# Split instead of unsplit weights for the second half of the K tiles in the first four projection groups of a hybrid decoder trunk

## The chip, the core and the metric

The kernel runs on one core of one Trainium2 chip. The metric is the device time of one execution in microseconds, the median of several executions. TensorE is called PE, its weight loads PEld, VectorE DVE, ScalarE ACT, GpSimd POOL, and SyncE SP; SP issues nearly all loads from HBM.

## What is computed

Two layers of a decoder trunk on a sequence of 256 tokens with a model width of 2048, in float32. Each layer normalizes and modulates its input, multiplies it with one wide input projection, mixes the heads in four different ways, projects back, and adds a gated feed-forward part. Only the start of layer 0 matters here:

```
mod = cond @ w_ada[l] + b_ada[l]
sh1, sc1, g1, sh2, sc2, g2 = jnp.split(mod[:, None, :], 6, axis=-1)
h = rms_norm(x, norm_gain[l, 0]) * (1.0 + sc1) + sh1
w_proj = w_in[l] if l == 0 else jnp.concatenate([w_in[l], vres_down[l - 1]], axis=1)
p = h @ w_proj
...
y_mix = jnp.concatenate([y_a, y_b, y_c, y_d], axis=-1) @ w_out[l]
x = x + g1 * y_mix
...
x = x + g2 * ((jax.nn.silu(gate) * up) @ ffn_w2[l])
```

`cond` is one vector, so `mod` is 12288 dot products of length 2048 per layer.

## The kernel before

The width of 2048 is cut into 16 K tiles of 128. For each K tile `h` exists in two forms. `hh` and `hl` are its high and low part in the fp32r type, made by ACT (`hh`) and DVE (`hl`); a product of two split operands is three fp32r matmuls (hh x hi, hl x hi, hh x lo). `u` is the unsplit h in float32, used for one float32 matmul in place of the three.

Weights come in *pieces* of 128 x 1024: two K tiles of a group of 512 output columns. An unsplit piece is loaded into a tile called `whole` and used as it lies. A split piece is loaded, two at a time, into a tile called `raw` (1 MB, three buffers); ACT copies it into `hi` (method `conv`), DVE subtracts to get `lo` (method `lower`). `hi` and `lo` have four buffers each, which the `whole` tiles share. `conv` for the piece three ahead is emitted at the first K tile of a piece (`LEAD` is 3), `lower` soon after:

```python
nc.scalar.activation(hi[:, :n], raw, AF.Copy)
...
nc.vector.tensor_tensor(lo, raw, hi[:, :n].bitcast(F32), ALU.subtract)
```

Layer 0 begins in `start_quads`, which multiplies while `h` is still being made. For each K tile of h, four tiles `ar` of 128 x 1024 of the modulation weights `wada` are loaded (two halves each for scale and shift; five buffers), DVE multiplies each with `cond` and sums (a *dot*, method `ada_dot`), adds the bias (two or three tiny operations on `mod`) and makes `u` from x; ACT adds the shift to `u` and makes `hh`; DVE makes `hl`. One dot is emitted every one to three K tiles of matmuls, or more when a K tile of h is asked for that isn't there yet. The three stages of `start_quads`, in order:

- Stage 1: four groups named in `ONE` on K tiles 0 to 7, unsplit. The result is parked in `sp`.
- Stage 2: the groups lo, k, r and v (`TWO`) on K tiles 0 to 7, split, one group after the other.
- Stage 3: the same four groups on K tiles 8 to 15, into the same four accumulators (`q`, `q`, `m`, `m`: two PSUM banks each). The pieces go round the four groups, two K tiles at a time. Unsplit pieces are taken four at a time (`g = 4`): the four groups on the first K tile, then on the second.

When a group ends, ACT and DVE shift it out of PSUM into `sh` tiles. After stage 3 come the narrow group lo2, the rest of the `ONE` groups (which are split), and the other groups, between which a planner lays the work of the head mixers. It orders by its own clocks per engine, so a change of one stage's operations also moves later rows against each other.

The engines run their instructions in the order in which the program emits them, and SP issues its loads in that order too, each one when its buffer is free. The recording helper makes every instruction appear under line 181.

Of the kernel before, what the change touches and what calls it, by code (L numbers as in the profile page):

```python
# [15 lines left out]
KT = D // 128  # L16
# [15 lines left out]
ONE, TWO, KA = ("q" + GROUPS[0], "k" + GROUPS[0], "v" + GROUPS[0], "q" + GROUPS[1]), ("lo", "k", "r", "v"), 8  # L32
# [5 lines left out]
def weight_plan():  # L38


    plan = []
    count = itertools.count()

    def put(src, l, groups, ks, nk=None, beside=False, whole=False):

        out = []
        for j, (name, cols) in enumerate(groups):
            n = sum(c for _, c in cols)
            k = nk or max(i for i in (2, 4, 8) if i * n <= 1024)
            i = next(count)  # L50
            out.append([dict(src=src, l=l, name=name, quad=i, k0=k0, nk=k, cols=cols, n=n, whole=j in whole if isinstance(whole, tuple) else whole)
                        for k0 in ks if k0 % k == 0])
        for g in zip(*out) if beside else out:
            plan.extend(g)

    for l in range(L):
        lo = 3 * GW
        g0 = lo + 192
        base = NIN - 9 * GW
        cols = dict(lo=[(lo, 96), (g0, 32), (lo + 96, 96), (g0 + 32, 32), (g0 + 64, 256)],  # L60
                    lo2=[(g0 + 320, 128)] + ([(NIN, 64)] if l else []),
                    k=[(GW, GW)], r=[(0, GW)], v=[(2 * GW, GW)])
        for g in GROUPS:
            i = "BCD".index(g)
            for w, t in enumerate("qkv"):
                cols[t + g] = [(base + (3 * i + w) * GW, GW)]
        allk = range(KT)
        if l == 0:
            one, two = [(n, cols[n]) for n in ONE], [(n, cols[n]) for n in TWO]
            put("in", l, one, range(KA), beside=True, whole=True)  # L70
            put("in", l, two, range(KA))
            put("in", l, two, range(KA, KT), beside=True, whole=True)
            put("in", l, [("lo2", cols["lo2"])], allk)
            put("in", l, one, range(KA, KT))
            put("in", l, [(n, c) for n, c in cols.items() if n not in ONE + TWO + ("lo2",)], allk)
        else:
            put("in", l, list(cols.items()), allk)
        outs = [(f"o{q}", [(q * 512, 512)]) for q in range(4)]
        for g in (outs[:2], outs[2:]):
            for i, part in enumerate(WO[:2]):  # L80
                put("w_out", l, g, part, whole=i in PLAIN[l])
        put("w_out", l, outs, WO[2], whole=2 in PLAIN[l])
        f0 = 0
        for c in CHUNKS:
            fs = [(f"f{p}", [(p * 128, 256), (DFF + p * 128, 256)]) for p in range(f0, f0 + c, 2)]
            if f0 == 0:
                put("w13", l, fs[:4], allk, beside=True)
                fs = fs[4:]
            put("w13", l, fs, allk)
            put("w2", l, [(f"p{q}", [(q * 512, 512)]) for q in range(4)], range(f0, f0 + c))  # L90
            f0 += c
    units, off, i = [], 0, 0
    while i < len(plan):
        m = i
        w = 0
        while m < len(plan) and plan[m]["whole"] == plan[i]["whole"] and w + plan[m]["nk"] * plan[m]["n"] <= (1024 if plan[i]["whole"] else UNIT):
            plan[m].update(unit=len(units), at=w)
            w += plan[m]["nk"] * plan[m]["n"]
            m += 1
        units.append((off, w, i, m))  # L100
        off += 128 * w
        i = m
    return plan, units, off
# [108 lines left out]
class Kern:  # L212
    def __init__(self, tc, nc, I, out, ctx, cfg):
# [14 lines left out]
        self.dr = en(tc.tile_pool(name="dr", bufs=1, space=bass.MemoryType.DRAM))  # L228
        self.uid = 0
        self.plan, self.units, _ = weight_plan()  # L230
        self.adae = getattr(self.nc, cfg.get("adae", "sync"))
        self.next_dma = self.next_conv = self.pos = 0
# [1594 lines left out]
def prepare(inp):  # L1827
# [5 lines left out]
    d["c"] = np.ascontiguousarray(g["c"])  # L1833
    d["wada"] = np.ascontiguousarray(g["w_ada"].transpose(0, 2, 1).reshape(L, 96, 128, D))
    plan, units, total = weight_plan()
    wst = np.empty(total, np.float32)
    src = {}
# [71 lines left out]
```

## Time and profile before

| | |
|---|---|
| median of 3 runs | 2596.36 us (2595.82 to 2599.79) |
| the profiled execution | 2601.3 us, of which the span of the trace is 2599.4 us |
| PE, DVE, ACT busy over the span | 97%, 70%, 44% |
| DMA over the span | 252 GB/s |
| stage 3 | from 140.6 to 196.6 us of the span |

The profiled execution took 1.9 us more than its span, and lies 4.9 us above the median of the runs. A busy PE isn't PE at its peak: matmuls overlap, so the distance from start to start is what one costs.

### The profile page before, as it was taken

The numbers are of one execution on the slowest core, as the hardware profiler recorded it, in microseconds if no ns is written. First come the engines' busy times: TensorE is split into PE (matmuls) and PEld (weight loads), VectorE is DVE, ScalarE is ACT, GpSimd is POOL, SyncE is SP. The second block draws the span as 40 slices with busy tenths as digits, with TensorE's granted clock in tenths as the row PEclk, the third lists the DMA queues.
The fourth block names the chain that finished last, engine by engine and source line by source line (L and its number), as shares of the span: only waits on it lengthen the run. The fifth ranks groups of instructions, "written<-read, shape, count | busy, mean of one in ns | idle before, by whom it ended". The sixth has DMA issues, their size and how long they took to land.

```text
span 2599.4 us, 37374 instructions
## 1 busy us (share of the span) xinstructions
PE 2522.2 (97%) x14550; PEld 2162.3 (83%) x14550; DVE 1810.8 (70%) x2934; ACT 1133.4 (44%) x1602; POOL 153.0 (6%) x270
## 2 busy tenths in 40 slices
PE   7999999999999999999999999999899999999998
PEld 4888888887888888888899998989788888888887
DVE  6766887859877887865567878889754455545555
ACT  2315445414444434433455454566444444444343
POOL 0001122010000000000020012100100000000001
PEclk9999999999999999999999999999899999999999
DMA  9895688878898888865577786787455555555553
GB/s 352 314 375 199 212 271 267 312 266 323 322 345 325 323 331 329 319 243 185 180 257 273 261 280 227 261 306 262 146 181 193 193 194 190 192 186 193 179 194 114
DMA packets 136019, 654.70 MB, mean 252 GB/s; under 512 B 18581, under 2 KB 24749, under 8 KB 88609
## 3 DMA queue, kind: packets, MB, share of 16 engines
q1 hardware_dynamic: 126306, 632.72, 67.1%
q0 software_dynamic: 8960, 18.55, 2.4%
q8 instruction: 114, 1.87, 0.3%
q10 hardware_dynamic: 576, 1.05, 0.1%
q14 instruction: 63, 0.52, 0.1%
HBM read 643.82 MB, written 10.77 MB: 252 GB/s over the span
## 4 chain that ended last, share of the span: by engine, by line
PE 89%; DMA 5%; DVE 4%; ACT 2%; issue 1%; POOL 0%; SPq 0%; DVEq 0%; ACTq 0%; POOLq 0%
PE q L181 75%; PE m L181 13%; DMA ar<-wada 2%; DVE ar L181 1%; DMA gb<-gate 1%; DVE lo L181 1%; DMA raw<-wst 0%; DVE x L181 0%; ACT hi L181 0%; PE st L181 0%; DMA XT<-scr 0%; DMA whole<-wst 0%; DVE rstd L181 0%; DVE out L181 0%; ACT sh L181 0%
## 5 line engine op out<-in xcount | busy, mean ns | idle before, releaser
L181 DVE TENSOR_TENSOR lo<-raw,hi 128x1024 fp32r<-128x1024 f32 (+1 forms) x742 | 904.4, 1226 | 504.7 <-ACT hi L181 504.2
L181 ACT ACTIVATE hi<-raw 128x1024 fp32r<-128x1024 f32 (+1 forms) x742 | 780.7, 1058 | 923.9 <-PE q L181 762.0
L181 DVE SCALAR_TENSOR_TENSOR ar<-ar,cond 128x1024 f32<-128x1024 f32 x384 | 464.2, 1223 | 54.4 <-DMA ar<-wada 53.6
L181 PE MATMUL q<-hi,hh 128*128 128x512 f32 x1456 | 456.0, 394 | 7.0 <-ACT hh L181 6.8
L181 PE MATMUL q<-lo,hh 128*128 128x512 f32 x1456 | 453.4, 393 | 0.0
L181 PE MATMUL q<-hi,hl 128*128 128x512 f32 x1456 | 450.6, 391 | 0.0
L181 PEld LDWEIGHTS q<-hi,hl 128*128 128x128 f32 x1456 | 274.3, 188 | 58.8 <-issue 0.4
L181 PEld LDWEIGHTS q<-hi,hh 128*128 128x128 f32 x1456 | 270.2, 189 | 62.7 <-ACT hh L181 7.9
L181 PEld LDWEIGHTS q<-lo,hh 128*128 128x128 f32 x1456 | 272.2, 188 | 57.3 <-issue 1.5
L181 PE MATMUL q<-hh,hi 128*128 128x256 f32 (+1 forms) x1040 | 176.2, 289 | 5.9 <-ACT hh L181 3.4
L181 PE MATMUL q<-hh,lo 128*128 128x256 f32 (+1 forms) x1040 | 177.0, 290 | 2.7 <-DVE lo L181 2.6
L181 PE MATMUL q<-hi,ah 128*128 128x512 f32 x576 | 178.3, 391 | 0.0
L181 PE MATMUL q<-lo,ah 128*128 128x512 f32 x576 | 178.2, 391 | 0.0
L181 PE MATMUL q<-hi,al 128*128 128x512 f32 x576 | 177.5, 389 | 0.0
L181 PE MATMUL q<-hl,hi 128*128 128x256 f32 (+1 forms) x1040 | 171.2, 284 | 0.0
L181 PEld LDWEIGHTS q<-hh,hi 128*128 128x128 f32 (+1 forms) x1040 | 145.8, 193 | 13.7 <-issue 5.7
L181 PEld LDWEIGHTS q<-hh,lo 128*128 128x128 f32 (+1 forms) x1040 | 145.4, 192 | 8.6 <-issue 3.5
L181 PEld LDWEIGHTS q<-hl,hi 128*128 128x128 f32 (+1 forms) x1040 | 144.8, 192 | 0.1
L181 POOL TENSOR_TENSOR sq<-sq,sq 128x256 f32<-128x256 f32 x44 | 36.2, 822 | 1680.6 <-ACT sq L181 1678.1
L181 PEld LDWEIGHTS q<-hi,al 128*128 128x128 f32 x576 | 108.1, 188 | 22.6
L181 PEld LDWEIGHTS q<-lo,ah 128*128 128x128 f32 x576 | 107.5, 188 | 22.0
L181 PEld LDWEIGHTS q<-hi,ah 128*128 128x128 f32 x576 | 107.4, 188 | 21.8
(270 smaller groups left out, 2644.1 us busy)
## 6 DMA issues: line engine op xcount, KB each, us to landing
raw<-wst SPq DMA_DIRECT2D x369, 1024.0 KB, 5.0
ar<-wada SPq DMA_DIRECT2D x384, 512.0 KB, 6.7
whole<-wst SPq DMA_DIRECT2D x64, 512.0 KB, 7.6
x<-xt SPq DMA_DIRECT2D x32, 128.0 KB, 4.0
bias<-bskew POOLq DMA_DIRECT2D x24, 128.0 KB, 6.9
bskew<-bscr POOLq DMA_DIRECT2D x4, 576.0 KB, 19.5
gb<-gb POOLq DMA_DIRECT2D x16, 128.0 KB, 5.9
xd<-x POOLq DMA_DIRECT2D x16, 128.0 KB, 5.9
```

The source lines that it names most:

```text
L181: return f(*a, **kw)
```

## The change

One flag falls. The pieces of stage 3 are split ones, as in stage 2; `beside=True` stays, so they still go round the four groups, each piece with its two K tiles.

```diff
             put("in", l, one, range(KA), beside=True, whole=True)
             put("in", l, two, range(KA))
-            put("in", l, two, range(KA, KT), beside=True, whole=True)
+            put("in", l, two, range(KA, KT), beside=True)
             put("in", l, [("lo2", cols["lo2"])], allk)
```

On PE, the first rows of stage 3, before. `u_564` and `u_792` are h on K tiles 8 and 9, the numbers behind `whole` those of the pieces of lo, k, r and v:

```order
L181 MATMUL q_213<-u_564,whole_923 128x256 x4
L181 MATMUL q_214<-u_564,whole_984 128x256 x4
L181 MATMUL m_215<-u_564,whole_1019 128x256 x2
L181 MATMUL m_216<-u_564,whole_1019 128x256 x2
L181 MATMUL m_217<-u_564,whole_1045 128x256 x2
L181 MATMUL m_218<-u_564,whole_1045 128x256 x2
L181 MATMUL q_213<-u_792,whole_923 128x256 x4
```

And now:

```order
L181 MATMUL q_213<-hh_565,hi_986 128x256 x4
L181 MATMUL q_213<-hl_634,hi_986 128x256 x4
L181 MATMUL q_213<-hh_565,lo_987 128x256 x4
L181 MATMUL q_213<-hh_793,hi_986 128x256 x4
L181 MATMUL q_213<-hl_846,hi_986 128x256 x4
L181 MATMUL q_213<-hh_793,lo_987 128x256 x4
L181 MATMUL q_214<-hh_565,hi_1023 128x256 x4
```

Three matmuls stand where one stood, and group lo takes both K tiles before group k starts.

On DVE, in the middle of stage 3, before: the four dots (`ar`) of K tile 12, its `u_1150` and `hl_1164`, with nothing else between them:

```order
L181 SCALAR_TENSOR_TENSOR ar_1083,mod_73<-ar_1083,cond 128x1024
L181 SCALAR_TENSOR_TENSOR mod<-mod_73,vecs 128x1
L181 SCALAR_TENSOR_TENSOR mod<-mod,vecs 128x1
L181 SCALAR_TENSOR_TENSOR ar_1092,mod_73<-ar_1092,cond 128x1024
L181 SCALAR_TENSOR_TENSOR ar_1099,mod_73<-ar_1099,cond 128x1024
L181 SCALAR_TENSOR_TENSOR mod<-mod_73,vecs 128x1
L181 SCALAR_TENSOR_TENSOR u_1150<-x_110,mod,rstd_200 128x256
L181 SCALAR_TENSOR_TENSOR ar_1112,mod_73<-ar_1112,cond 128x1024
L181 TENSOR_TENSOR hl_1164<-u_1150,hh_1151 128x256
```

The same K tile now (`u_1236`, `hl_1260`):

```order
L181 TENSOR_TENSOR lo_1202<-raw_1122,hi_1201 128x1024
L181 SCALAR_TENSOR_TENSOR ar_1120,mod_73<-ar_1120,cond 128x1024
L181 SCALAR_TENSOR_TENSOR ar_1141,mod_73<-ar_1141,cond 128x1024
L181 SCALAR_TENSOR_TENSOR mod<-mod_73,vecs 128x1
L181 SCALAR_TENSOR_TENSOR u_1236<-x_110,mod,rstd_200 128x256
L181 TENSOR_TENSOR lo_1242<-raw_1122,hi_1241 128x1024
L181 SCALAR_TENSOR_TENSOR ar_1162,mod_73<-ar_1162,cond 128x1024
L181 TENSOR_TENSOR hl_1260<-u_1236,hh_1237 128x256
```

Sixteen `lo` have come between the dots. `lo_1242` stands right behind `u_1236`.

On ACT, the same place, before:

```order
L181 ACTIVATE u_1102<-u_1102,mod 128x256
L181 ACTIVATE hh_1103<-u_1102 128x256
L181 ACTIVATE u_1150<-u_1150,mod 128x256
L181 ACTIVATE hh_1151<-u_1150 128x256
L181 ACTIVATE u_1190<-u_1190,mod 128x256
```

And now:

```order
L181 ACTIVATE hi_1201<-raw_1122 128x1024
L181 ACTIVATE u_1236<-u_1236,mod 128x256
L181 ACTIVATE hh_1237<-u_1236 128x256
L181 ACTIVATE hi_1241<-raw_1122 128x1024
L181 ACTIVATE hi_1281<-raw_1199 128x1024
```

The copy `hi_1241`, which PE and `lo_1242` need, stands behind `u_1236` and `hh_1237`, which need the dots of K tile 12. On SP, seven loads of 1 MB into `raw` stand where fourteen of 512 KB into `whole` stood ahead of the last `ar` of the stage; an eighth follows it.

## Rows read from the trace of the kernel before

**Rows 1.** Busy time by stretch: length, busy time (instructions), PE's granted clock, DMA share, GB/s.

```profile
98.00:140.60 42.60, 41.52 (x344) 41.12 (x343) 30.91 (x46) 16.59 (x20) 0.00 (x0) 1.00 0.72 263
140.60:196.60 56.00, 55.79 (x258) 48.33 (x256) 33.18 (x70) 9.73 (x19) 2.80 (x7) 1.00 1.02 399
```

**Rows 2.** The chain of waits, 98 to 220 us: start, length, what.

```profile
149.62 8.55 DMA ar<-wada
...
189.70 3.47 PE q L181 x16
193.19 0.48 ACT sh L181
...
218.17 1.94 PE q L181 x14
```

**Rows 3.** PE in order of time: start, length, operation, count, idle before and releaser.

```profile
140.16 0.64 PE L181 MATMUL m<-hh,lo 128*128 128x256 f32 x4
140.64 3.62 PE L181 MATMUL q<-u,whole 128*128 128x256 f32 x16
...
192.99 3.62 PE L181 MATMUL m<-u,whole 128*128 128x256 f32 x16
198.09 0.39 PE L181 MATMUL q<-hh,hi 128*128 128x256 f32 x1 [1.49 <-DVE sh L181]
```

**Rows 4.** DVE's groups, 136 to 187.5 us: count | busy, mean ns | idle before, releaser.

```profile
L181 DVE SCALAR_TENSOR_TENSOR ar<-ar,cond 128x1024 f32<-128x1024 f32 x21 | 25.4, 1221 | 13.5 <-DMA ar<-wada 13.5
L181 DVE SCALAR_TENSOR_TENSOR mod<-mod,vecs 128x1 f32<-128x1 f32 x16 | 3.2, 200 | 0.6
L181 DVE TENSOR_TENSOR hl<-u,hh 128x256 fp32r<-128x256 f32 x6 | 2.5, 422 | 1.0 <-ACT hh L181 1.0
```

**Rows 5.** DVE in order of time, stages 2 and 3.

```profile
99.90 3.50 DVE L181 TENSOR_TENSOR lo<-raw,hi 128x1024 fp32r<-128x1024 f32 x3 [1.97 <-ACT hi L181]
103.32 1.22 DVE L181 SCALAR_TENSOR_TENSOR ar<-ar,cond 128x1024 f32<-128x1024 f32 x1
...
113.48 1.23 DVE L181 TENSOR_TENSOR lo<-raw,hi 128x1024 fp32r<-128x1024 f32 x1 [3.59 <-ACT hi L181]
...
120.76 2.36 DVE L181 TENSOR_TENSOR lo<-raw,hi 128x1024 fp32r<-128x1024 f32 x2 [1.97 <-ACT hi L181]
...
132.54 1.23 DVE L181 TENSOR_TENSOR lo<-raw,hi 128x1024 fp32r<-128x1024 f32 x1 [3.22 <-ACT hi L181]
...
135.96 1.22 DVE L181 SCALAR_TENSOR_TENSOR ar<-ar,cond 128x1024 f32<-128x1024 f32 x1
...
183.18 0.43 DVE L181 TENSOR_TENSOR hl<-u,hh 128x256 fp32r<-128x256 f32 x1 [1.02 <-ACT hh L181]
```

**Rows 6.** ACT in order of time, one K tile of stage 2.

```profile
118.82 0.51 ACT L181 ACTIVATE u<-u,mod 128x256 f32<-128x256 f32 x1 [4.42 <-DVE u L181]
119.36 0.42 ACT L181 ACTIVATE hh<-u 128x256 fp32r<-128x256 f32 x1
119.69 1.99 ACT L181 ACTIVATE hi<-raw 128x1024 fp32r<-128x1024 f32 x2
```

**Rows 7.** PE in stage 1, two rounds of the same sixteen matmuls.

```profile
33.56 3.72 PE L181 MATMUL q<-u,whole 128*128 128x256 f32 x16 [1.56 <-ACT u L181]
...
84.29 5.41 PE L181 MATMUL q<-u,whole 128*128 128x256 f32 x16 [3.43 <-ACT u L181]
```

**Rows 8.** Busy time by stretch, as rows 1, around a wait of PE.

```profile
84.00:86.00 2.00, 1.71 (x4) 1.44 (x5) 0.34 (x1) 1.97 (x4) 0.00 (x0) 0.59 0.96 346
86.00:88.00 2.00, 2.00 (x6) 1.59 (x6) 1.22 (x2) 0.58 (x1) 0.00 (x0) 0.56 1.05 385
88.00:90.00 2.00, 2.00 (x10) 1.56 (x9) 1.36 (x2) 0.86 (x2) 0.00 (x0) 1.00 0.97 377
```

**Rows 9.** PE's two waits after stage 3.

```profile
218.17 0.74 PE L181 MATMUL q<-hh,lo 128*128 128x256 f32 x4 [2.64 <-DVE lo L181]
...
268.30 4.56 PE L181 MATMUL m<-sh,up 32*128 32x256 f32 x10 [3.42 <-DVE kar L181]
```

## The prediction, as put on record before the change was run

> **What bounds the kernel now.** The page first: PE is busy for 97% of the span, so time lost or won on PE stays lost or won to the end, unless a later wait of PE swallows it. The busy time by stretch comes next [rows 1]. In stage 3 PE is busy for 55.8 of 56.0 us at a granted clock of 1.00, DMA is full at 399 GB/s, DVE works 33.2 us and ACT 9.7 us. Whoever reads only this sees a PE-bound stage with two idle engines. The chain of waits corrects that: it enters stage 3 through PE, but also through a load of `ar` of 8.55 us [rows 2]. So behind PE a second chain runs nearly as late, that of h: loads of `ar`, dots on DVE, `u`, `hh`, `hl`. DVE's groups show it [rows 4]: of the stretch from the first dot of the stage (135.96 us) to the last `hl` (183.61 us) [rows 5], 47.6 us, DVE waited 13.5 us for `ar`, 1.0 for `hh` and 0.6 for small things, and worked 32.5 us. PE took the last K tile at about 189.7 us [rows 2], so h was ready some 6 us before it was needed. That is the whole slack.
>
> **The change part by part.** *PE.* Sixteen unsplit records follow each other in 3.46 us, and the stage has 256, so it costs 56 us (140.64 to 196.6, [rows 3]). Four split matmuls take 0.48 us from start to start [rows 3], so one piece on one K tile takes three times that, 1.44 us; 32 of these are 46.1 us. Taken alone that is a gain of 9.9 us, with an end at 186.7 us.
>
> *DVE.* Sixteen `lo` are added. Three in a row take 3.42 us until the next row starts, 1.14 us each [rows 5]: 18.2 us. With the 32.5 us there already, DVE has 50.7 us of work, more than PE's 46.1. DVE runs in its own order, and the order shows 14 of the 16 `lo` ahead of the last `u`, the first ahead of the first dot. So with no wait at all the last `u` is done at 135.96 + 32.5 - 0.4 (the last `hl`) + 14 x 1.14 = 184.1 us. The gain of 9.9 us is thereby excluded: DVE can't deliver the last K tile of h in time for it.
>
> *ACT.* Sixteen `hi` of about 1.0 us are added [rows 6] to an engine with 46 us to spare [rows 1]; hidden as work, not as order. Stage 2 already has the new pattern: a `u` on DVE, then `u` and `hh` on ACT, then `hi` on ACT, and DVE's next row is the `lo` of that `hi`. Twice DVE stood idle 1.97 us there [rows 5], which is what ACT needs for `u`, `hh` and `hi` [rows 6]. Before, nothing like it stands in stage 3; now three K tiles (10, 12 and 13) have `lo` straight behind `u`: 3 x 1.97 = 5.9 us. Last `u`: 190.0 us. Behind the waiting `lo` stand the next dots, and behind these, on SP, the loads that want their buffers.
>
> *Late data.* The bytes hardly change: `raw` in place of `whole`. But a dot that runs later frees its `ar` buffer later, and SP, which issues in order, now also waits for a `raw` buffer, which is free only after a `lo`. How much DVE then waits for loads is not in the trace. Below it is nothing: DVE, itself later, finds all `ar` landed. Above it is the 13.5 us that it waited in this stage [rows 4]. The nearest row is stage 2, which has this mix of dots and `lo`: no wait for `ar`, but 3.59 and 3.22 us for `hi` whose load was late [rows 5], 6.8 us at 263 GB/s. I take 6.8: the last `u` is done at 196.8 us, and `hh`, after `u` and `hh` on ACT [rows 6], 1.0 us later, at 197.8 us.
>
> *The end of the stage.* PE has by then done lo on K tile 14 and waits. Left are lo on K tile 15 and k, r and v on both, seven times 1.44 = 10.1 us: 207.9 us.
>
> *The clock.* A wait of that length has a price. After PE had waited 3.43 us, the granted clock stood at 0.59 and 0.56 for the next 4 us, near its lower level (1.2 GHz of 2.4) [rows 8], and the round that followed took 5.41 us in place of 3.72 [rows 7], 1.7 us more; after 2.64 us [rows 9] no loss shows. I add 1.7: 209.6 us, 13.0 us later than before. The Trainium skill ("TensorE: Matmul & The Clock Gate", section "HAM oscillation — how this bites in real kernels") goes further: in a loop in which every K tile waits for its data, PE falls back to the half clock in each wait and every K tile starts cold. By it all of the last 10.1 us would run at half speed, and the sum would be 8.4 us higher than by the rows. The rows agree that a wait costs clock, but show full speed again within the second round.
>
> *What comes back.* Before, the four groups ended within 6 us of each other, and PE then waited 1.49 us for lo's `sh` to leave its accumulator [rows 3] and 2.64 us for a `lo` that stood on DVE behind the shifting of all of them and the start of the mixers [rows 9]; the chain of waits runs through this from 193 to 218 us [rows 2]. Now each group ends 2.9 us after the one before it, lo 8.6 us ahead of the end, and most is shifted out by then: I take back 1.5 us of the first and 1.0 of the second. Bounds: nothing, and 4.1. Further on PE waits 3.42 us at 268 us [rows 9], behind POOL's loads and stores. In the new order the little matmul that starts POOL's table (`oh`, `rb`) stands about 4 us of PE's work earlier; I take back 1.5, between 0 and 3.4. After that the planner's rows are the same work in a shifted order; I count nothing for it, and some 3 us either way.
>
> Sum: +13.0 - 1.5 - 1.0 - 1.5 = +9.0 us. On the profiled execution, 2601.3 us, that is 2610.3; on the median of the runs, 2596.4, it is **2605.4 us**, which I forecast. A measurement tells 0.2% here, 5.2 us, from no change.
>
> **The rivals.**
> - *DVE never waits.* The loads come in time, and ACT and DVE overlap so that no `lo` waits: last `u` 184.1, `hh` 185.1, end 195.2 us, -1.4, and with the 4.0 us that come back -5.4: 2591.0 us. For it: DMA has fewer bytes per us to bring once DVE is the slower. Against it: the 1.97 us waits, which the order repeats. It is decided by the last `hh`: below about 190.5 us there the kernel gets faster. 0.11.
> - *Order costs, data doesn't.* The three waits of 1.97 us stay, no load is late, PE's wait is too short for the clock: 190.0 + 1.0 + 10.1 = 201.1, +4.5 - 4.0 = +0.5: 2596.9 us. For it: no dot waited for `ar` in stage 2. Against it: stage 2 asks for a dot once in some three K tiles of matmuls, about 10 in its 42 us, stage 3 for 21 [rows 4] in little more. 0.20.
> - *The loads stay as late as they were.* All 13.5 us remain beside the new work: 216.3, +19.7 - 4.0 = +15.7: 2612.1 us. For it: each late dot delays the buffer for a later one. Against it: DVE would be idle 19 us while fewer loads per us are wanted. 0.09.
> - *Cold to the end of the stage.* The last wait drops the clock until the stage ends: +9.0 + 8.4 = +17.4: 2613.8 us. For it: the drop itself [rows 8]. Against it: the recovery in the same rows. [...] 0.07.
>
> **How the numbers follow.** The forecast has the remaining 0.53, with 2600 to 2610 as its own range. Faster by over 0.2% is the first rival alone: 0.11. Within 0.2% are the second rival and a little of the forecast's lower end: 0.20 + 0.06 = 0.26. Slower: 0.63. From 2594.5 to 2613 the range leaves out the first rival and the upper half of the last ones, 0.18.
>
> **What would show it.** In the trace after, stage 3 still starts at 140.6 us and ends near 209. Four split matmuls still take 0.48 us, with PE busy well under 50 us of some 68. DVE's `ar` group shows far less than 13.5 us of waits for DMA, its `lo` group 10 to 15 us for ACT's `hi`. PE's longest wait is for `hh` of the last K tile, over 4 us, with a granted clock near half behind it. DMA falls clearly below 399 GB/s. The prediction is wrong if the last `hh` comes before 190 us, if PE waits in the stage less than 10 us in total, or if the waits at 218 and 268 us grow by more than they are taken to shrink.

## The result and the profile after

The changed kernel takes 2627.5 us (median of four runs, 2626.3 to 2632.7), the kernel before beside it 2598.1 (2595.8 to 2604.1): a ratio of 1.0102, 95% interval 1.0084 to 1.012. That is slower, as forecast, but by 29 us and not by 9, and 14.5 us above the upper end of the range. The profiled execution took 2626.4 us, its span 2624.7, so 25.3 us more than the span before. The ratio on record lies a little below the quotient of the two medians, 1.0113; versions are compared by their ratios from here on.

Busy time by stretch, in the columns of [rows 1]; the second stretch is stage 3, which now ends at 207.8 us and ended at 196.6:

```profile
98.00:140.60 42.60, 41.52 (x344) 41.11 (x343) 29.40 (x41) 17.91 (x22) 0.00 (x0) 1.00 0.76 278
140.60:207.80 67.20, 53.07 (x385) 51.45 (x384) 52.97 (x89) 24.81 (x35) 2.79 (x7) 0.90 0.82 300
```

PE is no longer full (53.1 of 67.2 us, at a mean granted clock of 0.90), DMA fell from 399 to 300 GB/s, and DVE went from 33 us of work to 53. The chain of waits through the stage (start, length, what) no longer runs through loads of `ar`. It is DVE and ACT handing work to each other, and in two places a load of `raw`; a stretch of PE from 165 to 169 us, left out here, belongs to it too:

```profile
150.61 7.22 DMA raw<-wst
157.91 1.07 ACT hi L181
159.00 1.23 DVE lo L181
...
162.69 0.49 DVE u L181
163.20 0.52 ACT u L181
163.74 0.42 ACT hh L181
164.16 0.95 ACT hi L181
...
178.81 8.24 DMA raw<-wst
187.14 1.07 ACT hi L181
188.23 1.23 DVE lo L181
...
192.19 1.14 DVE lo L181
193.33 1.15 DVE ar L181 x2
194.51 0.22 DVE mod L181
194.73 0.41 DVE u L181
195.16 0.52 ACT u L181
195.70 0.42 ACT hh L181
196.17 6.08 PE q L181 x36
```

SP issued these two loads of `raw` right behind loads of `ar` that had waited for DVE (issued at 150.19 and 178.29 us in the same chain). So DVE's lateness comes back to DVE as a late `hi`.

DVE's groups from 136 to 198 us, beside [rows 4]: the dots (`ar`) wait for nothing, where they waited 13.5 us for loads, and the new `lo` wait 10.4 us for ACT's high part:

```profile
L181 DVE SCALAR_TENSOR_TENSOR ar<-ar,cond 128x1024 f32<-128x1024 f32 x21 | 25.4, 1219 | 0.0
L181 DVE TENSOR_TENSOR lo<-raw,hi 128x1024 fp32r<-128x1024 f32 x15 | 18.4, 1224 | 11.5 <-ACT hi L181 10.4 <-PE q L181 1.1
```

PE in order of time, beside [rows 3] and [rows 9]. Four split matmuls take 0.48 us from start to start at full clock; after the wait of 4.46 us they take 0.81 to 0.86 for a while. The last rows are the wait for lo's accumulator and the two waits behind it:

```profile
196.17 0.73 PE L181 MATMUL q<-hh,hi 128*128 128x256 f32 x4 [4.46 <-ACT hh L181]
196.74 1.01 PE L181 MATMUL q<-hl,hi 128*128 128x256 f32 x4
...
198.41 1.06 PE L181 MATMUL q<-hh,hi 128*128 128x256 f32 x4
199.26 1.05 PE L181 MATMUL q<-hl,hi 128*128 128x256 f32 x4
...
207.35 0.64 PE L181 MATMUL m<-hh,lo 128*128 128x256 f32 x4
210.56 0.58 PE L181 MATMUL q<-hh,hi 128*128 128x256 f32 x1 [2.58 <-DVE sh L181]
...
231.64 0.74 PE L181 MATMUL q<-hh,lo 128*128 128x256 f32 x4 [2.19 <-DVE lo L181]
...
283.69 4.90 PE L181 MATMUL m<-sh,up 32*128 32x256 f32 x10 [7.91 <-DVE kar L181]
```

Put beside the same matmuls of the kernel before, these rows give a staircase. Stage 3 ends 11.2 us later. lo2 starts 12.5 us later (210.56 against 198.09, [rows 3]). The matmuls behind the wait for `kar` start 15.4 us later (283.69 against 268.30, [rows 9]). The rest of the 25 us comes behind that wait. So less than half of the loss lies in the stage that was changed. Held against the time of the same split matmul before, the kernel is 12.0 us behind at 258 us, 16.0 at 336, 23.2 at 698 and 25.3 at the end. What does the rest, and what sets stage 3's end? The experiments take these two apart. Their "order" is the order in which the planner writes the rows of each engine; it follows the planner's own clocks, and those stand elsewhere after a stage 3 of other operations.

### The profile page after: what moved, and what is told of

Same layout as the page of the kernel before. It is cut to its first block, busy times and chain, and to the rows that moved or that the text cites. A ratio compares the mean times of both kernels' runs of the same rounds, so it can differ in the third digit from the quotient of the medians.

```text
span 2624.7 us, 37677 instructions
## 1 busy us (share of the span) xinstructions
PE 2524.8 (96%) x14678; PEld 2168.5 (83%) x14678; DVE 1828.8 (70%) x2950; ACT 1149.2 (44%) x1618; POOL 152.6 (6%) x270
## 3 DMA queue, kind: packets, MB, share of 16 engines
q10 hardware_dynamic: 576, 1.05, 0.1%
## 4 chain that ended last, share of the span: by engine, by line
PE 81%; DVE 9%; DMA 7%; ACT 2%; issue 1%; SPq 0%; POOL 0%; DVEq 0%; ACTq 0%; POOLq 0%
PE q L181 70%; PE m L181 11%; DVE ar L181 3%; DMA ar<-wada 3%; DMA raw<-wst 2%; DVE lo L181 2%; DMA gb<-gate 1%; DVE x L181 1%; ACT hi L181 1%; PE st L181 0%; DMA x<-xt 0%; DVE iv L181 0%; DVE e L181 0%; DVE xt L181 0%; DVE rstd L181 0%
## 5 line engine op out<-in xcount | busy, mean ns | idle before, releaser
L181 DVE TENSOR_TENSOR lo<-raw,hi 128x1024 fp32r<-128x1024 f32 x758 | 923.3, 1227 | 509.0 <-ACT hi L181 500.0
L181 ACT ACTIVATE hi<-raw 128x1024 fp32r<-128x1024 f32 x758 | 797.0, 1058 | 923.3 <-PE q L181 765.0
L181 PE MATMUL q<-hh,hi 128*128 128x256 f32 x1104 | 189.4, 292 | 15.2 <-ACT hh L181 11.6
L181 PE MATMUL q<-hh,lo 128*128 128x256 f32 x1104 | 188.4, 291 | 4.1 <-DVE lo L181 4.0
L181 PE MATMUL q<-hl,hi 128*128 128x256 f32 x1104 | 184.2, 287 | 3.0 <-DVE hl L181 3.0
L181 PEld LDWEIGHTS q<-hh,hi 128*128 128x128 f32 x1104 | 156.6, 195 | 23.9 <-ACT hh L181 12.6
L181 PEld LDWEIGHTS q<-hh,lo 128*128 128x128 f32 x1104 | 155.9, 194 | 9.9 <-DVE lo L181 5.2
L181 PEld LDWEIGHTS q<-hl,hi 128*128 128x128 f32 x1104 | 156.4, 195 | 3.2 <-DVE hl L181 3.2
```

The lines of the kernel that those rows point to most:

```text
L181: return f(*a, **kw)
```

## The experiments

Twelve runs were made; each ratio is to the kernel before on the same chip. One median is not to be held against another chip's: the kernel before itself read 2598 to 2603 us there. To hold the order fixed, a run sets the planner's clocks and the ready times of its tiles and jobs at the end of stage 3 to fixed numbers, those of the changed kernel ("new" in the table) or of the kernel before ("old"):

```diff
             spill = self.start_quads(hs, hbegin, hend, done_q)
+            self.settle(SETTLED)
             self.ada_on = True
```

| run | stage 3 | order behind it | other edit | ratio | interval |
|---|---|---|---|---|---|
| changed kernel | split | new | | 1.0102 | 1.0084 to 1.0120 |
| e12 again | split | new | | 1.0109 | 1.0091 to 1.0126 |
| e1 | whole | new | | 1.0051 | 1.0033 to 1.0069 |
| e2 | split | old | | 1.0047 | 1.0031 to 1.0063 |
| e3 | split | new | gate's stores | 1.0084 | 1.0067 to 1.0102 |
| e4 | split, no `lo` | new | | 1.0050 | 1.0030 to 1.0069 |
| e5 | split | new | half of `lo` on POOL | 1.0084 | 1.0067 to 1.0101 |
| e6 | split | new | dot first | 1.0058 | 1.0042 to 1.0075 |
| e7 | half split | new | | 1.0050 | 1.0033 to 1.0066 |
| e8 | whole | old | gate's stores | 0.9987 | 0.9975 to 1.0000 |
| e9 | whole | new | gate's stores | 1.0010 | 0.9996 to 1.0023 |
| e10 | split | old | gate's stores, dot first | 1.0015 | 1.0002 to 1.0028 |
| e11 | half split | old | gate's stores, dot first | 1.0008 | 0.9996 to 1.0021 |

**Stage or order (e1, e2).** The two halves of the change were put in one at a time. e1 keeps whole weights and takes the new order; e2 splits and takes the old one.

> The kernel before, whole weights in stage 3, but from lo2 on every engine's rows stand in the order of the changed kernel (the planner's clocks are set at the end of stage 3 to what they were in the changed kernel). Theory A (the 14 us lost behind stage 3 come from work that starts late, whatever the order): as the kernel before, 2598 us, within 4. Theory B (the order that the planner makes from its shifted clocks is the worse one): 8 to 14 us slower, 2606 to 2612.

> The changed kernel, split weights in stage 3, but from lo2 on every engine's rows stand in the order of the kernel before. Theory A: no gain, 2624 to 2631 us. Theory B: the 8 to 14 us come back, 2613 to 2619 us, and what is left over the kernel before is stage 3 with its 11 us.

Measured 1.0051 (2614.2 us) and 1.0047 (2612.5 us): theory B. With the kernel before as 1, the two add up to 1.0098, and both together measured 1.0102 and 1.0109. So the stage costs some 12 us and the order some 13, and they hardly touch each other. In e1, whose stage 3 is the one of before, PE waits 6.92 us for `kar`, and PE, then DVE, show what for:

```profile
262.31 0.65 PE L181 MATMUL m<-kq,sh 64*64 64x128 f32 x16
269.89 4.90 PE L181 MATMUL m<-sh,up 32*128 32x256 f32 x10 [6.92 <-DVE kar L181]
274.23 1.35 PE L181 MATMUL q<-hh,hi 128*128 128x256 f32 x4
```

```profile
267.22 0.43 DVE L181 TENSOR_TENSOR bh<-a,dall 128x256 f32<-128x256 f32 x1 [9.03 <-DMA gb<-gate]
```

`bh` takes the buffer of a `gate` tile, which is free only when the tile's store to DRAM has landed. That store is queued on POOL behind the four copies `bskew` of 576 KB. POOL in the same run:

```profile
242.03 4.32 POOL L181 DMA_DIRECT2D bskew<-bscr  x4 [6.75 <-DMA bscr<-bm]
246.30 0.63 POOL L181 DMA_DIRECT2D gb<-gate  x1
```

It was issued at 246.3 us and landed at 267.2. In the kernel before, the chain of waits has 19.7 us for the same store. The new order makes DVE's `bh` only 1.3 us later (265.88 in the chain of waits before), but gives PE 1.9 us less work ahead of the place, so that PE stands there from 263.0 us and not from 264.9. A wait of 3.4 us became one of 6.9. The half clock behind it is no part of the difference, for it stands in both kernels: the ten matmuls `sh,up` take 4.34 us to the next row in e1, at a granted clock of 0.50, and 3.99 in the kernel before (268.30 to 272.29, and half clock to 275 us); at full clock, 250.9 us in e1, ten take 2.27. That it is the place behind the copies which makes the store late, and not POOL's queue as such, fits the other stores: in e1 the eight `gate` stores land 4.7 us after their issue in the median, the four copies 17.8.

**Gate's stores (e3, e8, e9).** The store of `gate`, made by ACT, is issued by ACT; nothing else of any engine's work moves (the edit holds for both layers).

```diff
-            nc.gpsimd.dma_start(R["gb"][j, :, 1, :], g[:])
+            nc.scalar.dma_start(R["gb"][j, :, 1, :], g[:])
```

> The changed kernel with the four stores of gate to DRAM issued on ACT's queue and not on POOL's, where they stand behind the bskew copies. If the wait of 7.9 us for kar at 283 us comes from that queue (bh takes the slot of the gate tile), the wait falls below 3 us, the half clock behind it goes, and the time falls by 5 to 9 us, to 2618 to 2622. If the slot is only the last of several late things, the wait stays above 5 us and the time moves by less than 3 us.

> The kernel before with the changed kernel's order from lo2 on (it cost 13 us over the kernel before) and the stores of gate on ACT's queue. If the order costs its time at the wait for kar and in the half clock behind it, about 7 of the 13 us come back: 1.000 to 1.003 times the kernel before. If that wait is a symptom and the order costs elsewhere, less than 3 us come back: 1.004 to 1.006.

> The kernel before with the four stores of gate issued on ACT's queue. If the wait for kar (3.4 us) and the half clock behind it come from POOL's queue as in the changed kernel, 3 to 6 us faster, 2593 to 2596 us; if another wait takes its place, within 2 us of 2599.

In e9, the new order without the long wait, 1.0051 fell to 1.0010: 11 us come back. DVE and PE there, and PE's clock behind the wait (columns of [rows 1]):

```profile
257.75 0.42 DVE L181 TENSOR_TENSOR bh<-a,dall 128x256 f32<-128x256 f32 x1
261.93 0.43 DVE L181 TENSOR_TENSOR kh<-sh,dall 128x256 f32<-128x256 f32 x1 [3.77 <-DMA gb<-gate]
```

```profile
263.63 3.50 PE L181 MATMUL m<-sh,up 32*128 32x256 f32 x10 [1.24 <-DVE kar L181]
```

```profile
266.00:268.00 2.00, 2.00 (x9) 1.75 (x8) 2.00 (x8) 0.38 (x1) 0.91 (x6) 0.50 0.51 191
```

The wait shrank by 5.7 us; the clock fell to 0.50 all the same.

In the changed kernel (e3) the wait falls from 7.9 to 1.9 us and the rows behind it start 6.9 us earlier, 7.8 from the next group on, and stay so to some 1560 us, with 4.3 left at the end; by the ratios the time moved by 4.7 us against the first measurement of the changed kernel and 6.5 against the second, near the lower end of what was expected. The wait behaved as expected, the clock did not: it still fell to 0.50 behind the shorter wait (278 to 280 us). In the kernel before (e8) 3.4 us come back, with an interval that reaches to no change. By its ratio it is the fastest version of the study.

So e9 must be held against e8, which has the same stores, and not against the kernel before. Between these two the new order still costs 0.0023 of the time, some 6 us (about 1 to 11 by the two intervals). By these ratios about 7 of the order's 13 us hang on that store; the others do not. The traces show where those lie. Behind stage 3 all versions run the same sequence of `q` matmuls, so the same one can be found in each (start in us):

| the same `q` matmul | before | e8 | e1 | e9 |
|---|---|---|---|---|
| first of lo2 | 198.09 | 199.23 | 198.81 | 198.22 |
| ahead of the wait for `kar` | 258.32 | 260.98 | 257.55 | 256.97 |
| behind it | 336.01 | 335.61 | 338.25 | 330.96 |
| further on | 697.58 | 698.87 | 706.71 | 700.96 |

Over the wait for `kar` e1 loses 3 us against the kernel before, while e9 gains 4 and e8 gains 3: with the store moved, the new order costs nothing at this place. But from the third matmul to the fourth the kernel before takes 361.6 us and e9 370.0:

```profile
336.01:697.58 361.57, 349.36 (x2150) 296.79 (x2148) 289.76 (x631) 147.48 (x283) 32.53 (x54) 0.99 0.83 292
```

```profile
330.96:700.96 370.00, 353.34 (x2149) 298.47 (x2148) 293.51 (x639) 147.16 (x283) 34.75 (x60) 0.98 0.82 290
```

The five traces with the old order take 360 to 363 us here, the nine with the new one 368 to 372, whatever their stage 3 and wherever `gate`'s stores are issued. These 7 to 8 us of the new order do not hang on that store; e9 comes out level with the kernel before because the store's place had cost that kernel time too.

**What sets stage 3's end (e4, e6, e5, e7).** All four keep the new order. e4 leaves out the sixteen subtractions (a second edit, not shown, lets PE read `hi` in place of `lo`):

```diff
-            self.nc.vector.tensor_tensor(lo, raw, hi[:, :n].bitcast(F32), ALU.subtract)
+            if not 32 <= i < 48:
+                self.nc.vector.tensor_tensor(lo, raw, hi[:, :n].bitcast(F32), ALU.subtract)
```

> The changed kernel without DVE's 16 subtractions of stage 3; the third pass multiplies by the high part again, so TensorE's work is the same and the result leaves out the low products of these eight K tiles. If DVE's sum sets the end of stage 3 (the prediction's step), the last K tile comes about 18 us earlier, at most back to the loads' pace of the kernel before: stage 3 ends at 190 to 196 us and not at 207.8, and the time is 2606 to 2614 us or less. If the waits of PE for ACT's rounding and the half clock set it, the stage ends at 200 or later and the time falls by less than 8 us.

The stage ends at 191.8 us, 16 us earlier, and the time falls to 1.0050, the cost of the order alone (lo2 starts 4.3 us earlier than in e1, but in the profiled runs little of this is left at the end). TensorE does the same work, so it was DVE's. With DVE free, the bound is the old one, the loads of `ar`, in DVE's group:

```profile
L181 DVE SCALAR_TENSOR_TENSOR ar<-ar,cond 128x1024 f32<-128x1024 f32 x20 | 24.5, 1223 | 12.2 <-DMA ar<-wada 12.1
```

e6 leaves DVE all its work and changes only what stands first, the next dot or the subtraction that waits for ACT:

```diff
-                    self.lower()
                     if due >= 1.0:
                         due -= 1.0
                         more()
+                    self.lower()
```

(In stage 3 only; the condition that sees to it is left out here.)

> The changed kernel, its order from lo2 on kept; in stage 3 the dot and the scaling of the next K tile stand ahead of a piece's subtraction on DVE, so that ACT has time to round the high part. If the waits of DVE for ACT's high part (3 x 1.97 us and six of 0.5 to 1.7) delay the last K tile, they go and the stage ends 5 to 9 us earlier, 2618 to 2622 us. If DVE's work alone sets it and the waits only fill gaps, less than 3 us, 2625 to 2630 us.

1.0058: 11 to 13 us of the changed kernel's 26 to 28, some more than expected. In its trace stage 3 ends 4.5 us earlier, DVE's `lo` wait 5.4 us for ACT and not 10.4, and lo2 starts 7.3 us earlier because the wait of 2.58 us for lo's `sh` is gone too; with it went the half clock behind it. So the waits in DVE's order were a cost of their own beside its sum.

e5 moves every second subtraction to POOL, which had 2.8 us of work in the stage.

```diff
-            self.nc.vector.tensor_tensor(lo, raw, hi[:, :n].bitcast(F32), ALU.subtract)
+            e = self.nc.gpsimd if 32 <= i < 48 and i % 2 else self.nc.vector
+            e.tensor_tensor(lo, raw, hi[:, :n].bitcast(F32), ALU.subtract)
```

> The changed kernel, its order from lo2 on kept, with every second subtraction of stage 3 (8 of 16) done by POOL, which is idle there. POOL's 128x256 operation of two tensors took 0.82 us, so about 3.3 us for one of these, 26 us in a stage of 67. If DVE's sum sets the end of stage 3, about 8 x 1.14 = 9 us and part of the order waits go: the stage ends at 196 to 200 us and not at 207.8, and the time is 2616 to 2621 us. If PE's waits for ACT set it, or if POOL and DVE slow each other down by as much, the time stays within 4 us of 2627.5.

1.0084 (2624.4 us): by the ratios 5 to 6 us below the changed kernel, with intervals that overlap. The trace decides: the stage ended at 209.3 us, no earlier than with all on DVE. POOL and DVE at the same time:

```profile
176.92 5.18 POOL L181 TENSOR_TENSOR lo<-raw,hi 128x1024 fp32r<-128x1024 f32 x2 [6.36 <-ACT hi L181]
```

```profile
177.55 4.58 DVE L181 SCALAR_TENSOR_TENSOR mod<-mod,vecs 128x1 f32<-128x1 f32 x2
182.05 1.21 DVE L181 TENSOR_TENSOR lo<-raw,hi 128x1024 fp32r<-128x1024 f32 x1
```

Two operations on one column, 0.41 us together elsewhere, took 4.58 us, until POOL was done. Over the stage the sixteen `mod` rows took 11.3 us in place of 3.2. The eight `lo` taken from DVE came back as time in which it was shut out.

e7 splits the last four K tiles alone.

```diff
-            put("in", l, two, range(KA, KT), beside=True)
+            put("in", l, two, range(KA, 12), beside=True, whole=True)
+            put("in", l, two, range(12, KT), beside=True)
```

> The changed kernel, its order from lo2 on kept, but split weights in the last four K tiles of stage 3 only; K tiles 8 to 11 use whole weights as before. If the cost goes with the number of subtractions, half of the 13 us of stage 3 remain: 2620 to 2622 us. If 8 x 1.14 = 9 us of DVE work fit into the 13.5 us that DVE waited for loads in the kernel before, while PE saves 8 x 0.62 = 5 us, stage 3 costs nothing and the time is that of the kernel before with the new order or less, 2609 to 2615 us.

1.0050, as e1 with no split at all. DVE still waits for loads, so eight subtractions find room in what were waits; but PE's 5 us less of work buy nothing either, since the last K tile is no earlier (PE waits 5.36 us for it, and the stage ends at 199.0 us):

```profile
L182 DVE SCALAR_TENSOR_TENSOR ar<-ar,cond 128x1024 f32<-128x1024 f32 x20 | 24.3, 1220 | 10.5 <-DMA ar<-wada 10.5
```

**All mends together (e10, e11), and the control.** e10 is the changed kernel with the dot first, the old order and gate's stores on ACT; e11 the same with the half dose.

> The changed kernel with all three mends: the dot ahead of the subtraction in stage 3, the order of the kernel before from lo2 on, the stores of gate on ACT's queue. If the three costs stand beside each other: 13 us of stage 3 less 5 to 9, and 3 less at kar: 1.000 to 1.003 times the kernel before. If they overlap (what one gives back the next wait takes), 1.004 or more.

> Split weights in the last four K tiles of stage 3 only, with the same three mends. If DVE's spare time takes the eight subtractions and the loads still set the last K tile, stage 3 ends where it did in the kernel before, and the time is that with the gate stores on ACT's queue: 0.997 to 0.999 times the kernel before. If TensorE's 5 us less of work count, 0.995 to 0.997. If eight subtractions still delay the last K tile, 1.000 or more.

> The changed kernel once more, on the chip of the three runs beside it: 1.009 to 1.012 times the kernel before, as measured.

e10 measured 1.0015 and e12, on its chip, 1.0109: some 24 us of the loss are undone, and the split still gains nothing. e11 measured 1.0008, above the 0.997 to 0.999 expected: in its trace PE waits 3.2 us for the last `hh` and 1.1 for a `lo` in stage 3, which the kernel before does not, and the wait for `lo` at 218 us grew from 2.64 to 3.53. No version with split weights in this stage beat the kernel before, and held against e8, which has the same stores, e10 costs some 7 us and e11 some 5.

## Why the prediction was wrong, and where it was right

**Stage 3: right.** *PE alone, -9.9 us*, excluded as a gain because of DVE: e4 shows that DVE's subtractions set the end, e7 that less work on PE does not move it. *DVE, last `u` at 184.1 us without waits; three waits of 1.97 us; 6.8 us of late data*: the trace has no wait for `ar`, three waits of exactly 1.97 us, and 5.1 us of other waits ahead of the last `u` (0.68, 0.49, 1.12 and 1.68 for `hi`, 1.13 for PE's buffer). 184.1 + 5.9 + 5.1 = 195.1 us, and the last `u` is done at 195.1; forecast 196.8. The 6.8 us, a size borrowed from stage 2, had the right kind and the wrong amount: the waits of 0.68, 1.12 and 1.68 us are for `hi` whose `raw` came late, 3.5 us, and the other 1.6 come from the order of the rows and from PE. *From `hh` to the end 10.1 us and 1.7 for the clock*: 196.17 to 207.83, 11.7. The stage ended at 207.8; forecast 209.6.

**The clock.** After that longest wait it fell to half and came back some 4.5 us later, as the sum had it; stretch by stretch:

```profile
196.00:198.00 2.00, 1.83 (x11) 1.84 (x12) 1.33 (x2) 2.00 (x3) 0.00 (x0) 0.70 0.73 307
198.00:200.00 2.00, 2.00 (x11) 2.00 (x11) 1.85 (x3) 0.59 (x3) 0.00 (x0) 0.50 0.00 0
200.00:202.00 2.00, 2.00 (x18) 2.00 (x18) 1.14 (x2) 1.31 (x2) 0.00 (x0) 0.95 0.69 209
```

But the sentence "after 2.64 us no loss shows" did not carry over: the clock also fell after a wait of 2.69 us at 165 us (to 0.52 from 166 to 168 us) and after 3.19 and 2.95 us at 175 and 178 us (to 0.50 from 178 to 182 us). The rule cited from the Trainium skill ("TensorE: Matmul & The Clock Gate", section "HAM oscillation — how this bites in real kernels"), that waits in a K loop put PE back to the half clock, agrees with the trace in this: three of the stage's waits did. It did not stay cold to the end of the stage, and that rival is out; that it would was the prediction's own extension of that section, which speaks of the K tile behind a wait.

**What comes back, -4.0 us: wrong.** This part failed first. The wait for lo's `sh` was to shrink by 1.5 us, since lo would be out 8.6 us before the end; it grew from 1.49 to 2.58, and lo2, at half clock to begin with, ended another 1.4 us later. The evacuation was not late for want of time but for its place: on DVE the `sh` rows stand behind `lo` rows that wait for ACT. e6, which moves those, starts lo2 with no such wait; e2, with the old order behind the stage, has 1.05 us there. The wait at 218 us shrank by 0.4, not 1.0. The wait at 268 us was to shrink by 1.5 because the table's matmul stands earlier; it grew from 3.4 to 7.9, which the prediction itself had named as a sign that it is wrong.

**"The same work in a shifted order; I count nothing for it, and some 3 us either way": wrong, and the largest term.** e1 measured it: 13 us. About 7 of them hang on one wait for one buffer behind POOL's copies (e9 held against e8). The prediction looked at the start of POOL's chain, which moved earlier, and not at who waits at its end and with how much PE work ahead. The rest lies where it did not look at all: from 336 to 698 us every trace of the new order takes some 7 us more for the same PE work. With the order of the kernel before, the split costs about what the prediction's stage costs (e2, 1.0047, 12 us), which would have been within the range, near its upper end.

**The rivals.** None named what happened. *DVE never waits* and *order costs, data doesn't* ended stage 3 too early; *the loads stay as late* and *cold to the end* gave later times, 2612 and 2614 us, for causes that the trace excludes: no dot waited for its load, and the clock came back.

**What stays open.** What makes the 7 us between 336 and 698 us was not taken apart. Some 2 of them are two waits of PE for `lo` that the kernel before does not have (1.39 us at 657 and 0.80 at 669 us of the changed kernel, 1.35 and 0.70 in e9; e8 has one of 1.17); no run tried them, or the rest, alone. By the ratios e3 gains 5 to 7 us where e9 gains 11, which is within the intervals; by the traces both are 7 to 8 us ahead at the matmul at 336 us. Up to 2 us more go in layer 1, where such losses come and go between runs.

## What to carry to other kernels

Less work on the engine that looks full is worth nothing while a second chain runs 6 us behind it, and an engine that is 60% busy is not free: sum its work in its own order, with what each row waits for, as stage 3's end came out within 2 us that way. Where a planner decides the order from its own clocks, a local change is two changes; hold the downstream order fixed and measure each, before either is priced at nothing. When a mend helps the changed kernel, give it to the kernel before as well, and compare these two: else what it gives to both looks like a loss undone. And look for buffers whose release hangs on a store in a queue of large copies: here one changed line gave back some 7 us at the wait.

## What the runs showed of the hardware

POOL's subtractions shut DVE out. In e5, while POOL subtracted (2.4 to 2.8 us each, where 3.3 was estimated from a smaller operation), operations of DVE with two operands in SBUF that started behind POOL's were not done before POOL was: 4.58 us for 0.41, and dots of 3.37 and 3.43 us for 1.22. The Trainium skill ("SBUF — State Buffer", section "Who interferes with whom") says that a DVE instruction with two SBUF inputs contends with a GpSimd instruction that reads SBUF, and that the order of issue decides which of the two blocks; these rows agree.

How long the clock stays down behind a wait does not go by the length of the wait. In the changed kernel the granted clock stood at 0.50 for some five us after the 7.9 us wait for `kar`, about as long as after the 4.46 us one; PE ran ten small matmuls on 32 rows there, and full clock came back with the large ones behind them:

```profile
284.00:288.00 4.00, 4.00 (x10) 2.71 (x10) 3.73 (x10) 0.00 (x0) 0.76 (x1) 0.50 0.27 66
288.00:290.00 2.00, 2.00 (x14) 1.91 (x13) 0.00 (x0) 0.53 (x2) 0.70 (x6) 0.76 0.03 8
290.00:292.00 2.00, 2.00 (x19) 2.00 (x19) 1.05 (x1) 0.92 (x1) 0.10 (x3) 1.00 0.18 66
```

In the kernel before, after 3.42 us of waiting at the same place, it stayed down for some seven us, through the ten small matmuls and three us of large ones (268.3 to 275.2). And it fell without any wait: there PE was busy throughout from 220 to 236 us, ran matmuls on 96, 8 and 32 rows from 225 us on, and had a clock of 0.50 at 232 us:

```profile
232.00:234.00 2.00, 2.00 (x7) 1.56 (x6) 1.81 (x5) 0.00 (x0) 0.00 (x0) 0.50 0.64 172
```

What of this comes from the waits and what from the small matmuls, no run here separates.
